# FFN of an encoder kernel: one 512-column product for both parts of the moving operand, and a down projection in two halves of its columns

## Chip, cores and metric

The kernel runs on one core of a Trainium2 chip. The metric is the device time of one execution in microseconds (us), the median of three runs.

## What is computed

An encoder of four layers over 256 tokens of width 1024. Every layer is a half-step SwiGLU FFN, a mixer (attention, convolution, Fourier, gated linear attention in turn) and a second half-step FFN, each with an RMS norm ahead of it; a last norm ends it. The change is in the FFN, which runs eight times:

```python
D_MODEL, SEQ, DEPTH, D_FF = 1024, 256, 4, 2816
def _swiglu(h, w1, w3, w2):
    return (jax.nn.silu(h @ w1) * (h @ w3)) @ w2
for i in range(DEPTH):
    h = h + 0.5 * _swiglu(_rmsnorm(h, norm_g[i, 0]), ffn_w1[i, 0], ffn_w3[i, 0], ffn_w2[i, 0])
    h = h + mix(_rmsnorm(h, norm_g[i, 1]))
    h = h + 0.5 * _swiglu(_rmsnorm(h, norm_g[i, 2]), ffn_w1[i, 1], ffn_w3[i, 1], ffn_w2[i, 1])
return _rmsnorm(h, final_norm_g)
```

## The kernel before

Activations lie transposed on the chip, features on the partitions and 256 tokens along the free dimension. Each float32 matrix operand is split into a high part and a low part (type fp32r), and a product of two of them is three matmuls: high times high, high times low, low times high (`mm3`). The weight is the stationary operand (128x128), the activation the moving one (256 columns), and the three accumulate into the same 256 columns of a PSUM bank.

Weights come in blocks of 1 MB (128x2048), in the order in which they are used (`plan`). SP starts the transfer of a block into one of four `raw` buffers; `split_block` makes the high part `wh` on ACT (L151) and the low part `wl` on DVE (L154), into one of four pairs. `done` notes that a block's products are issued, and `pump(n)` then splits up to n further blocks into the pairs that come free. The order of each engine's work is the order in which the code calls it; nothing reorders it.

An FFN (`ffn`) walks over 11 groups of 256 of the 2816 hidden features. For a group i it multiplies x by a block of w1 (`A`) and one of w3 (`B`), 96 matmuls each at 48 per block, the result of a block being one of four rotating PSUM banks `ab`. `evac_a` multiplies A by R (1/rms of each token) on DVE (L441) and takes silu on ACT (L442); `evac_b` multiplies B by R (L447), multiplies the two (L448) and splits the result into `gh` (ACT, L517) and `gl` (DVE, L518). The down projection of group i-1 follows group i (`DOWN_AFTER`; the last three come at the end), 48 matmuls into four banks D that hold all 1024 output columns through the whole FFN. `down_final` finishes the four D banks one after the other, and `close_pair` adds each to the residual h (L261), scales it by the norm's gain into the next stage's x (`normed`) and squares it (`square`).

R needs the sum over all of x, so it comes late: `stats(True)` sums on PE in the middle of group 0 (L389 reads it), and `newton_rsqrt` takes three Newton steps of three DVE instructions (L354 to L356). After the first two DVE instructions of it two blocks are split, the low part of one on DVE, that of the other on POOL (`eng=nc.gpsimd`). The stage of the convolution mixer uses the same `stats(True)`.

Of the kernel before, what the change touches and what calls it, by code (L numbers as in the profile page):

```python
# [20 lines left out]

DOWN_AFTER = {i: i - 1 for i in range(1, NG - 2)}
DOWN_AFTER[NG - 1] = NG - 3
# [17 lines left out]
class Enc:  # L41
    def __init__(self, ctx, tc, a, stages):
        self.ctx, self.tc, self.nc, self.a = ctx, tc, tc.nc, a
        self.stages = stages
        P = lambda name, bufs=1, **kw: ctx.enter_context(tc.tile_pool(name=name, bufs=bufs, **kw))
        self.const = P("const")
        self.wp = P("wp")
        self.hp = P("hp")
        self.ev = None
        self.ps = P("ps", space=PSUM)  # L50
        self.dram = P("dram", space=bass.MemoryType.DRAM)
        self.nm = 0

# [8 lines left out]
    def ab(self):  # L62
        return self.ps.tile([128, 512], F32, tag="ab", name=self.name("ab"), bufs=4)

    def dbank(self, j):
        return self.ps.tile([128, 512], F32, tag=f"D{j}", name=self.name(f"D{j}"), bufs=1)
# [6 lines left out]

    def mm3(self, out, l, r, start, stop, passes=(0, 1, 2)):
        (lh, ll), (rh, rl) = l, r
        for p in passes:
            self.mm(out, (lh, lh, ll)[p], (rh, rl, rh)[p], start and p == 0, stop and p == 2)
# [6 lines left out]
    def plan(self):  # L84
# [58 lines left out]
    def split_block(self, between=None, eng=None):  # L143
# [5 lines left out]
        wh = self.sb(self.wp, [128, 2048], F32R, "wh", NW)  # L149
        wl = self.sb(self.wp, [128, 2048], F32R, "wl", NW)  # L150
        self.nc.scalar.activation(wh, raw, AF.Copy)  # L151
        if between:
            between()
        (eng or self.nc.vector).tensor_tensor(wl, raw, f32(wh), ALU.subtract)  # L154
        self.wsp[b] = (wh, wl)
        self.dma_block()

    def take(self, key):
# [3 lines left out]
        wh, wl = self.wsp.pop(b)  # L162
        r = lambda t: t.rearrange("p (a b) -> p a b", a=self.blocks[b][1])
        return r(wh), r(wl)
# [17 lines left out]
    def setup(self):  # L182
# [9 lines left out]
        for b in first:  # L192
            self.raw[b] = self.sb(self.wp, [128, 2048], F32, "raw", NR)
            self.wsp[b] = (self.sb(self.wp, [128, 2048], F32R, "wh", NW), self.sb(self.wp, [128, 2048], F32R, "wl", NW))
# [19 lines left out]
        for j in range(4):  # L214
            self.normed(j)
            s = slice(512 * j, 512 * j + 512)
            for b in first:
                wh, wl = self.wsp[b]
                self.split(self.raw[b][:, s], wh[:, s], wl[:, s])
# [6 lines left out]
        while self.nsplit < NW:  # L226
            self.split_block(eng=nc.gpsimd)
# [19 lines left out]
    def close_pair(self, j, P, scale, bias=None):  # L247
        nc = self.nc
        h = self.h[j]
        P3 = P.rearrange("p (c n) -> p c n", c=2)  # L250
        if self.unperm:
            assert bias is None
            hn = self.sb(self.ev, [128, 2, 256], F32, "sl", 2)
            for c in range(2):
                nc.vector.scalar_tensor_tensor(hn[:, c].rearrange("p (m a) -> p a m", a=4),
                                               P3[:, c].rearrange("p (a m) -> p a m", a=4), float(scale),
# [3 lines left out]
        elif bias is None:  # L260
            nc.vector.scalar_tensor_tensor(h, P3, float(scale), h, ALU.mult, ALU.add)  # L261
        else:
            for c in range(2):
                nc.vector.scalar_tensor_tensor(h[:, c], P3[:, c], bias[c], h[:, c], ALU.add, ALU.add)
# [8 lines left out]
    def normed(self, j, h=None):  # L273
# [3 lines left out]
        if self.nstage < len(self.stages):  # L277
            xh = self.sb(self.hp, [128, 2, 256], F32R, f"xh{j}")
            xl = self.sb(self.hp, [128, 2, 256], F32R, f"xl{j}")
# [5 lines left out]
            self.xn[j] = (xh, xl)  # L285
        else:

            y = f32(self.sb(self.hp, [128, 2, 256], F32R, f"xh{j}"))
# [5 lines left out]
    def square(self, j, h=None, before_split=None):  # L294
# [17 lines left out]
        if j == 3:  # L312
# [5 lines left out]
            if self.row_norm():  # L318
                self.nsq = [self.sb(self.hp, [128, 256], F32R, "R", 2) for _ in range(2)]
                self.split(self.acc[:, 0], *self.nsq)  # L320
# [16 lines left out]
    def xk(self, k, t=None):  # L337
        xh, xl = self.x[k // 2]
        if t is None:
            return xh[:, k % 2, :], xl[:, k % 2, :]  # L340
        return xh[:, k % 2, 128 * t:128 * t + 128], xl[:, k % 2, 128 * t:128 * t + 128]

    def newton_rsqrt(self, y, r, shape, tag, bufs=2, pool=False):
# [37 lines left out]
    def stats(self, row=False, scale=1.0):  # L381

        if row:
# [6 lines left out]
            self.newton_rsqrt(y, self.R, [128, 256], "nR", 1, self.nstage > 0)  # L390
            return
# [24 lines left out]

    def ffn(self, l, s):
# [4 lines left out]
        g = {}  # L422

        def up(i, names, hook={}):

            ws = [self.take((n, i)) for n in names]
            ps = [self.ab() for _ in names]
            for k in range(8):
                for w, p in zip(ws, ps):
                    for c in range(2):  # L430
                        sl = slice(128 * c, 128 * c + 128)
                        self.mm3(p[:, 256 * c:256 * c + 256], (w[0][:, k, sl], w[1][:, k, sl]), self.xk(k),
                                 start=k == 0 and c == 0, stop=k == 7)
                if k in hook:
                    hook[k]()
            self.done(len(names))
            return ps

        def evac_a(A):
            sl = self.sb(self.ev, [128, 2, 256], F32, "sl", 2)  # L440
            nc.vector.tensor_tensor(sl, self.v2(A), self.Rb(), ALU.mult)  # L441
            nc.scalar.activation(sl, sl, AF.Silu)  # L442
            return sl

        def evac_b(i, sl, B):
            br = self.sb(self.ev, [128, 2, 256], F32, "br", 2)
            nc.vector.tensor_tensor(br, self.v2(B), self.Rb(), ALU.mult)  # L447
            nc.vector.tensor_tensor(br, sl, br, ALU.mult)  # L448
            gh = self.sb(self.ev, [128, 2, 256], F32R, "gh", 3)
            gl = self.sb(self.ev, [128, 2, 256], F32R, "gl", 3)  # L450
            self.split(br, gh, gl)
            g[i] = (gh, gl)

        self.down_begin()
        first = self.nstage == 0
        A0, B0 = up(0, ("w1", "w3"), {7 if first else 4: lambda: self.stats(True)})
        for i in range(1, NG):
            A, = up(i, ("w1",))
            if i == 1:
                s0 = []  # L460
                self.pump(1, between=lambda: s0.append(evac_a(A0)), eng=nc.gpsimd if first else None)
                evac_b(0, s0[0] if s0 else evac_a(A0), B0)
            sl = evac_a(A)
            self.pump()
            if i == 4 and pre:
                self.pre = pre()
            B, = up(i, ("w3",))
            evac_b(i, sl, B)
            self.pump()
            if i in DOWN_AFTER:  # L470
                self.down_add(self.take(("w2", DOWN_AFTER[i])), g.pop(DOWN_AFTER[i]))
                self.done()
                if i < NG - 1:
                    self.pump()
        w = [self.take(("w2", i)) for i in (NG - 2, NG - 1)]
        self.down_final([(w[0], g[NG - 2]), (w[1], g[NG - 1])], 0.5)
        self.done(2)
        self.pump_end()
        self.close_stage(st)

# [7 lines left out]
    def dmm(self, w, g, d, k, stop=False, passes=(0, 1, 2)):  # L488
        if self.D4 is None:
# [4 lines left out]
                 (w[0][:, k, 128 * d:128 * d + 128], w[1][:, k, 128 * d:128 * d + 128]),  # L494
                 (g[0][:, k], g[1][:, k]), start=self.dfirst[j], stop=stop, passes=passes)
# [20 lines left out]
    def split(self, src, hi, lo):  # L516
        self.nc.scalar.activation(hi, src, AF.Copy)  # L517
        self.nc.vector.tensor_tensor(lo, src, f32(hi), ALU.subtract)  # L518
# [38 lines left out]
    def mix1(self):  # L557
# [12 lines left out]
        def pw1(i, names=("pa", "pg"), hook={}):  # L570
            ws = [self.take((n, i)) for n in names]
            ps = [self.ab() for _ in names]
            for k in range(8):
                for w, p in zip(ws, ps):
                    for c in range(2):
                        sl = slice(128 * c, 128 * c + 128)
                        self.mm3(p[:, 256 * c:256 * c + 256], (w[0][:, k, sl], w[1][:, k, sl]), self.xk(k),
# [78 lines left out]
        A0, G0 = pw1(0, hook={4: lambda: self.stats(True)})  # L656
# [84 lines left out]
        nn = self.sb(ev, [128, 4, 2, 256], F32R, "zs", 3)  # L741
        for i in range(4):
            if i < 2:
                hi, lo = (self.sb(self.hp, [128, 2, 256], F32R, f"x{t}{i}") for t in "hl")
            else:
                hi, lo = nn[:, 2 * i - 4], nn[:, 2 * i - 3]
# [9 lines left out]
            if i:  # L756
                for c in range(2):
                    self.split(zc[i][:, c], hi[:, c], lo[:, c])
            g.append((hi, lo))
# [20 lines left out]
    def mix2(self):  # L780
# [10 lines left out]
        def s1(g, banks):  # L791
            for t in range(2):
                for kk in range(2):
                    self.mm3(banks[t][:, 0:260], self.xk(2 * g + kk, t), tuple(half(w, kk) for w in cs),
                             start=kk == 0, stop=kk == 1)
            return banks

        def e1(g, banks):
            for t in range(2):
                h = self.sb(self.ev, [128, 260], F32R, f"a{g}{t}h")  # L800
                l = self.sb(self.ev, [128, 260], F32R, f"a{g}{t}l")
# [3 lines left out]
                ab[g][t] = (h, l)  # L805

        def s2(j):
# [3 lines left out]
            for c in range(2):  # L811
                for t in range(2):
                    for q in range(2):
# [3 lines left out]
                        h, l = ab[j][t]  # L817
                        self.mm3(p[:, 256 * c:256 * c + 256], (h[:, o:o + 128], l[:, o:o + 128]),
                                 (cs[0][:, t, r], cs[1][:, t, r]), start=n == 0, stop=t == 1 and q == 1)
# [688 lines left out]
```

## Time and profile before

| | us |
|---|---|
| median of three runs (2006.0 to 2008.27) | 2007.27 |
| the profiled execution, its own time | 2007.91 |
| its span, first to last instruction | 2006.1 |
| PE busy | 1959.9 |
| DVE busy | 1280.1 |
| ACT busy | 891.0 |

The profile page gives busy time by engine. A matmul's row is longer than the distance between the starts of two neighbours, since one begins while the last still drains; so the pace of PE is read from starts, not from durations. An idle time in a row of the timeline stands in brackets with the engine and line that ended it. PEclk in a table of stretches is the share of the full clock that was granted.

### The profile page before, as it was taken

The numbers are of one execution on the slowest core, as the hardware profiler recorded it, in microseconds if no ns is written. First come the engines' busy times: TensorE is split into PE (matmuls) and PEld (weight loads), VectorE is DVE, ScalarE is ACT, GpSimd is POOL, SyncE is SP. The second block draws the span as 40 slices with busy tenths as digits, with TensorE's granted clock in tenths as the row PEclk, the third lists the DMA queues.
The fourth block names the chain that finished last, engine by engine and source line by source line (L and its number), as shares of the span: only waits on it lengthen the run. The fifth ranks groups of instructions, "written<-read, shape, count | busy, mean of one in ns | idle before, by whom it ended". The sixth has DMA issues, their size and how long they took to land.

```text
span 2006.1 us, 36900 instructions
## 1 busy us (share of the span) xinstructions
PE 1959.9 (98%) x16496; PEld 1926.2 (96%) x16496; DVE 1280.1 (64%) x1396; ACT 891.0 (44%) x921; POOL 90.2 (4%) x65
## 2 busy tenths in 40 slices
PE   7999999999999999899999999999999999999998
PEld 7999999999999997699999999999999999999998
DVE  6655667755675567775557655765576556767554
ACT  4433545543444443544334434443344445754433
POOL 2000000000060000000001000000010000001000
PEclk9999999999999999899999999999999999999999
DMA  6555533455445434145544553455446553334551
GB/s 233 213 188 186 185 145 127 166 191 181 156 180 202 178 143 163 51 179 192 184 161 181 190 189 127 156 202 188 175 152 227 184 185 148 127 127 168 192 186 43
DMA packets 48671, 338.59 MB, mean 169 GB/s; under 512 B 5568, under 2 KB 5744, under 8 KB 8192
## 3 DMA queue, kind: packets, MB, share of 16 engines
q1 hardware_dynamic: 47952, 335.11, 45.8%
q8 instruction: 129, 2.11, 0.4%
q0 software_dynamic: 560, 1.12, 0.2%
q14 instruction: 30, 0.25, 0.0%
HBM read 335.16 MB, written 1.05 MB: 168 GB/s over the span
## 4 chain that ended last, share of the span: by engine, by line
PE 89%; DVE 7%; ACT 2%; issue 1%; DMA 1%; SPq 0%; DVEq 0%; ACTq 0%
PE ab L69 57%; PE D L69 31%; DVE wl L154 2%; DVE nRt L354 1%; DVE zc L643 1%; ACT wh L151 1%; DMA raw<-in_ffn_w_dram 0%; DVE R L356 0%; DVE nRu L355 0%; PE D L72 0%; DVE nRu L348 0%; DMA h<-in_x_dram 0%; PE ab L72 0%; DVE R L518 0%; ACT zc L753 0%
## 5 line engine op out<-in xcount | busy, mean ns | idle before, releaser
L154 DVE TENSOR_TENSOR wl<-raw,wh 128x2048 fp32r<-128x2048 f32 x305 | 696.7, 2294 | 409.7 <-ACT wh L151 409.4
L69 PE MATMUL ab<-xh,wh 128*128 128x256 f32 x3200 | 911.9, 285 | 7.7 <-ACT wh L517 7.7
L69 PE MATMUL ab<-xh,wl 128*128 128x256 f32 x3200 | 909.3, 284 | 6.2 <-DVE wl L154 6.2
L69 PE MATMUL ab<-xl,wh 128*128 128x256 f32 x3200 | 908.9, 284 | 0.0
L151 ACT ACTIVATE wh<-raw 128x2048 fp32r<-128x2048 f32 x315 | 595.2, 1904 | 111.5 <-issue 84.9
L69 PEld LDWEIGHTS ab<-xh,wh 128*128 128x128 f32 x3200 | 617.9, 193 | 13.7 <-ACT wh L517 7.7
L69 PEld LDWEIGHTS ab<-xh,wl 128*128 128x128 f32 x3200 | 617.5, 193 | 6.9 <-DVE wl L154 6.6
L69 PEld LDWEIGHTS ab<-xl,wh 128*128 128x128 f32 x3200 | 617.9, 193 | 0.0
L69 PE MATMUL D<-gh,wh 128*128 128x256 f32 x1408 | 396.9, 282 | 6.5 <-ACT gh L517 6.5
L69 PE MATMUL D<-gl,wh 128*128 128x256 f32 x1408 | 400.3, 284 | 1.9 <-DVE gl L518 1.9
L69 PE MATMUL D<-gh,wl 128*128 128x256 f32 x1408 | 399.2, 284 | 0.0
L69 PEld LDWEIGHTS D<-gh,wh 128*128 128x128 f32 x1408 | 269.1, 191 | 7.5 <-ACT gh L517 7.5
L69 PEld LDWEIGHTS D<-gl,wh 128*128 128x128 f32 x1408 | 265.3, 188 | 3.0 <-DVE gl L518 2.9
L69 PEld LDWEIGHTS D<-gh,wl 128*128 128x128 f32 x1408 | 265.8, 189 | 0.0
L442 ACT ACTIVATE sl<-sl 128x512 f32<-128x512 f32 x88 | 55.6, 632 | 349.8 <-DVE sl L441 349.7
L517 ACT ACTIVATE gh<-br 128x512 fp32r<-128x512 f32 x88 | 55.6, 632 | 338.1 <-DVE br L448 338.1
L441 DVE TENSOR_TENSOR sl<-ab,R 128x512 f32<-128x512 f32 x88 | 60.6, 689 | 78.2 <-PE ab L69 77.5
L154 POOL TENSOR_TENSOR wl<-raw,wh 128x2048 fp32r<-128x2048 f32 x10 | 51.6, 5164 | 1216.1 <-ACT wh L151 774.6
L518 DVE TENSOR_TENSOR gl<-br,gh 128x512 fp32r<-128x512 f32 x88 | 61.4, 698 | 61.4 <-ACT gh L517 61.4
L282 ACT ACTIVATE xh<-h,cols 128x256 fp32r<-128x256 f32 x88 | 39.9, 500 | 73.9 <-DVE h L261 61.8
L447 DVE TENSOR_TENSOR br<-ab,R 128x512 f32<-128x512 f32 x88 | 60.6, 688 | 13.5 <-PE ab L69 13.5
L448 DVE TENSOR_TENSOR br<-sl,br 128x512 f32<-128x512 f32 x88 | 61.4, 697 | 4.9 <-ACT sl L442 1.4
(446 smaller groups left out, 1495.4 us busy)
## 6 DMA issues: line engine op xcount, KB each, us to landing
raw<-in_ffn_w_dram SPq DMA_DIRECT2D x262, 1024.0 KB, 4.8
raw<-in_attn_w_qk_dram SPq DMA_DIRECT2D x12, 1024.0 KB, 4.8
raw<-in_conv_w_pw_dram SPq DMA_DIRECT2D x12, 1024.0 KB, 4.8
raw<-in_gla_w_in_dram SPq DMA_DIRECT2D x12, 1024.0 KB, 4.9
raw<-in_attn_w_v_dram SPq DMA_DIRECT2D x6, 1024.0 KB, 4.8
raw<-in_fnet_w_dram SPq DMA_DIRECT2D x4, 1024.0 KB, 4.8
raw<-in_gla_w_o_dram SPq DMA_DIRECT2D x4, 1024.0 KB, 4.8
raw<-in_ffn_w_dram SPq DMA_DIRECT2D x8, 256.0 KB, 6.5
```

What stands on the lines that cost most here:

```text
L69: return self.nc.tensor.matmul(out, lhsT, rhs, start=start, stop=stop, skip_group_check=True)
L151: self.nc.scalar.activation(wh, raw, AF.Copy)
L154: (eng or self.nc.vector).tensor_tensor(wl, raw, f32(wh), ALU.subtract)
L282: nc.scalar.activation(xh[:, c], h[:, c], AF.Copy, scale=g[c])
L354: nc.vector.tensor_tensor(t, r, r, ALU.mult)
L441: nc.vector.tensor_tensor(sl, self.v2(A), self.Rb(), ALU.mult)
L442: nc.scalar.activation(sl, sl, AF.Silu)
L447: nc.vector.tensor_tensor(br, self.v2(B), self.Rb(), ALU.mult)
L448: nc.vector.tensor_tensor(br, sl, br, ALU.mult)
L517: self.nc.scalar.activation(hi, src, AF.Copy)
L518: self.nc.vector.tensor_tensor(lo, src, f32(hi), ALU.subtract)
L643: nc.vector.scalar_tensor_tensor(o, x, w, o, ALU.mult, ALU.add)
```

## The change

A weight's high part is loaded once and multiplies both parts of x (or of g) in one matmul of 512 moving columns, whose result is a high half and a low half of one PSUM bank; the low part times the high x adds 256 columns into the high half (`wide`). The two halves are added when the bank is read: ACT copies one half to SBUF (`parts`), DVE adds the other (`add`). A block of 256 features thus takes two banks where it took one. PSUM is two fixed halves of four banks; w1 has two banks (PA) and w3 two (PB), and the down projection has the other four, which is half of its columns. So the gated values `g` of all 11 groups stay on the chip (11 buffers), the first 512 columns are accumulated between the groups, two groups to a block, and the last 512 after them, into the four banks of PA and PB; then the roles of the halves are swapped (`lower`). `w2` is laid out for it in the host's arrays, still 11 blocks of 1 MB.

`R` is no longer needed to free a bank, so the Newton steps are spread between other instructions (`steps`). Silu's input and output are both multiplied by R, so w3's result isn't. POOL splits no blocks any more. `close_pair` adds two halves, one after the other. The other stages use the same banks through `ab` and `dbank`, and `mm3` as before.

```diff
@@ class Enc
     def ab(self):
-        return self.ps.tile([128, 512], F32, tag="ab", name=self.name("ab"), bufs=4)
+        self.nab = (self.nab + 1) % 4
+        while self.nab in self.held:
+            self.nab = (self.nab + 1) % 4
+        return self.bank(self.lower, self.nab)
+    def two(self, half, n):
+        return self.banks[half][n].rearrange("p (c q n) -> p c q n", c=2, q=2)
+    def pair(self, pool, shape, tag, bufs=1):
+        return self.sb(pool, [shape[0], 2, *shape[1:]], F32R, tag, bufs)
@@ def plan
-                    if i in DOWN_AFTER:
-                        add(("w2", DOWN_AFTER[i]), w2[DOWN_AFTER[i]], 2)
-                for i in (NG - 2, NG - 1):
-                    add(("w2", i), w2[i], 2)
+                    if i and i % 2 == 0:
+                        add(("w2", 0, i // 2 - 1), w2[i // 2 - 1], 4)
+                add(("w2",), w2[2 * NP], 2)
+                for i in range(NP):
+                    add(("w2", 1, i), w2[NP + i], 4)
@@ def setup
-        while self.nsplit < NW:
-            self.split_block(eng=nc.gpsimd)
+        self.pend = NW - self.nsplit
@@ def close_pair
-            nc.vector.scalar_tensor_tensor(h, P3, float(scale), h, ALU.mult, ALU.add)
+            for p in P:
+                nc.vector.scalar_tensor_tensor(h, p, float(scale), h, ALU.mult, ALU.add)
@@ def newton_rsqrt
-        if pool:
-            self.pump(1)
-            self.pump(1, eng=nc.gpsimd)
-        for n in range(3):
+        def step():
             nc.vector.tensor_tensor(t, r, r, ALU.mult)
             nc.vector.scalar_tensor_tensor(u, t, -0.5, y, ALU.mult, ALU.mult)
             nc.vector.scalar_tensor_tensor(r, u, 1.5, r, ALU.add, ALU.mult)
+        for _ in range(3 - later):
+            step()
+        return [step] * later
@@ def ffn
+    def wide(self, p, c, w, k, x, start, stop):
+        self.mm(p[:, c, 0], w[:, 1, k], x[:, 0], start, False)
+        self.mm(p[:, c], w[:, 0, k], x, False, stop)
...
+        def parts(P, tag):
+            t = self.sb(self.ev, [128, 2, 256], F32, tag, 2)
+            nc.scalar.activation(t, P[:, :, 1], AF.Copy)
+            return t
+        def add(t, P):
+            nc.vector.tensor_tensor(t, t, P[:, :, 0], ALU.add)
...
+        for n, ks in enumerate(cuts):
+            if n == len(cuts) - 1:
+                if not first:
+                    self.pump(1)
+                up(wa, PA, ks[:2])
+                if first:
+                    break
+                steps = self.stats(True)
+                up(wa, PA, ks[2:])
+            else:
+                up(wa, PA, ks)
+                up(wb, PB, ks)
+        self.done()
+        sl0 = parts(PA, "sl")
+        add(sl0, PA)
+        up(wb, PB, ks)
+        self.done()
...
+        steps.pop(0)()
+        br0 = parts(PB, "br")
+        steps.pop(0)()
+        add(br0, PB)
+        self.pump(held)
+        steps.pop(0)()
         for i in range(1, NG):
-            A, = up(i, ("w1",))
+            take_up("w1", i, PA)
+            sl = parts(PA, "sl")
             if i == 1:
...
+            else:
+                self.pump(1, between=lambda: (add(sl, PA), times_r(sl)))
+                silu(sl)
...
+            take_up("w3", i, PB)
+            br = parts(PB, "br")
+            self.pump(1, between=lambda: (times_r(sl), add(br, PB)))
+            gate(i, sl, br)
+            if i % 2 == 0:
+                p = i // 2 - 1
+                if i == NG - 1:
+                    break
+                self.half_add(self.take(("w2", 0, p)), [g[2 * p], g[2 * p + 1]], 0, p == 0)
...
+        p = NP - 1
+        self.half_add(self.take(("w2", 0, p)), [g[2 * p], g[2 * p + 1]], 0)
+        w = self.take(("w2",))
+        self.begin_close()
+        for j in range(2):
+            self.half_mm(w, [g[NG - 1]], 0, j, stop=True)
+            self.half_close(0, j)
+        self.lower = 1 - self.lower
+        for j in range(2):
+            self.half_mm(w[:, :, :, 512:], [g[NG - 1]], 1, j, start=True)
...
+        for p in range(NP):
+            self.pump(1)
+            w = self.take(("w2", 1, p))
+            if p < NP - 1:
+                self.half_add(w, [g[2 * p], g[2 * p + 1]], 1)
+        for j in range(2):
+            self.half_mm(w, [g[2 * p], g[2 * p + 1]], 1, j, stop=True)
+            self.half_close(1, j)
```

Three places show what moves; all three are in the second FFN of the third layer. First PE, at the start of the w1 block of group 1; `xh`, `xl`, `wh`, `wl` are the parts of x and of the block, `x` and `w` the pairs. Before:

```order
L69 MATMUL ab_15666<-xh_1594_15410,wh_15609 128x256
L69 MATMUL ab_15666<-xl_1595_15411,wh_15609 128x256
L69 MATMUL ab_15666<-xh_1594_15410,wl_15610 128x256
L69 MATMUL ab_15666<-xh_1594_15410,wh_15609 128x256
L69 MATMUL ab_15666<-xl_1595_15411,wh_15609 128x256
L69 MATMUL ab_15666<-xh_1594_15410,wl_15610 128x256
```

After:

```order
L81 MATMUL P_69<-x_949_11762,w_12154 128x256
L81 MATMUL P_69<-x_949_11762,w_12154 128x512
L81 MATMUL P_69<-x_949_11762,w_12154 128x256
L81 MATMUL P_69<-x_949_11762,w_12154 128x512
L81 MATMUL P_69<-x_949_11762,w_12154 128x256
L81 MATMUL P_69<-x_949_11762,w_12154 128x512
```

Three matmuls of 256 columns became one of 256 and one of 512.

Second DVE, from where it reads the sum of squares. Before, from L389 on (the POOL split stands beside L354 on POOL's own row):

```order
L389 TENSOR_SCALAR R_15599<-D_1616_15601 128x256
L348 TENSOR_SCALAR nRu_15606<-R_15599 128x256
L349 TENSOR_SCALAR R_15600<-nRu_15606 128x256
L154 TENSOR_TENSOR wl_15610<-raw_15215,wh_15609 128x2048
L354 TENSOR_TENSOR nRt_15605<-R_15600 128x256
L355 SCALAR_TENSOR_TENSOR nRu_15606<-nRt_15605,R_15599 128x256
L356 SCALAR_TENSOR_TENSOR R_15600<-nRu_15606,R_15600 128x256
```

After (L170 is the low part of a block, L465 is `add`):

```order
L170 TENSOR_TENSOR w_12051<-raw_11841,w_12051 128x2048
L406 TENSOR_SCALAR R_12064<-P_71 128x256
L363 TENSOR_SCALAR nRu_12070<-R_12064 128x256
L364 TENSOR_SCALAR R_12065<-nRu_12070 128x256
L465 TENSOR_TENSOR sl_12081<-sl_12081,P_69 128x512
L367 TENSOR_TENSOR nRt_12069<-R_12065 128x256
L368 SCALAR_TENSOR_TENSOR nRu_12070<-nRt_12069,R_12064 128x256
L369 SCALAR_TENSOR_TENSOR R_12065<-nRu_12070,R_12065 128x256
```

One split moved ahead of the sum, and reading PA moved in between.

Third DVE again, in group 1, with what follows the Newton steps. Before:

```order
L441 TENSOR_TENSOR sl_15718<-ab_15537,R_15600 128x512
L154 TENSOR_TENSOR wl_15716<-raw_15335,wh_15715 128x2048
L447 TENSOR_TENSOR br_15724<-ab_15538,R_15600 128x512
L448 TENSOR_TENSOR br_15724<-sl_15718,br_15724 128x512
L518 TENSOR_TENSOR gl_15728<-br_15724,gh_15727 128x512
L441 TENSOR_TENSOR sl_15731<-ab_15666,R_15600 128x512
```

After (L468 is `times_r`, L474 the gate, L623 the low part of g):

```order
L465 TENSOR_TENSOR sl_12149<-sl_12149,P_69 128x512
L468 TENSOR_TENSOR sl_12081<-sl_12081,R_12065 128x512
L468 TENSOR_TENSOR sl_12149<-sl_12149,R_12065 128x512
L170 TENSOR_TENSOR w_12154<-raw_11915,w_12154 128x2048
L468 TENSOR_TENSOR sl_12081<-sl_12081,R_12065 128x512
L474 TENSOR_TENSOR br_12103<-sl_12081,br_12103 128x512
L623 TENSOR_TENSOR g_12163<-br_12103,g_12163 128x512
L170 TENSOR_TENSOR w_12166<-raw_11952,w_12166 128x2048
L468 TENSOR_TENSOR sl_12149<-sl_12149,R_12065 128x512
L465 TENSOR_TENSOR br_12203<-br_12203,P_70 128x512
L170 TENSOR_TENSOR w_12205<-raw_12054,w_12205 128x2048
```

Between two reads of PA and PB there now stand two splits and five other instructions, where `ab` gave each block a bank of its own.

## Rows read from the trace of the kernel before

**Rows 1.** The page: span, and each engine's busy time with its instructions.

```profile
span 2006.1 us, 36900 instructions
PE 1959.9 (98%) x16496; PEld 1926.2 (96%) x16496; DVE 1280.1 (64%) x1396; ACT 891.0 (44%) x921; POOL 90.2 (4%) x65
```

**Rows 2.** The page: shares of the chain that ended last.

```profile
PE 89%; DVE 7%; ACT 2%; issue 1%; DMA 1%; SPq 0%; DVEq 0%; ACTq 0%
```

**Rows 3.** That chain in order of time: start us, us, engine and tile, instructions.

```profile
376.04 7.39 PE D L69 x47
...
400.70 11.51 PE ab L69 x96
```

**Rows 4.** Timeline of PE in the fourth mixer: start us, us, what.

```profile
1714.73 0.39 PE L69 MATMUL ab<-la00l,lst 128*128 128x512 f32 x1
...
1715.43 0.60 PE L72 MATMUL ab<-ident,kT 128*128 128x128 f32 x4
...
1716.10 0.40 PE L69 MATMUL D<-la01l,lst 128*128 128x512 f32 x1
...
1716.80 0.28 PE L69 MATMUL D<-tri,la00h 128*128 128x256 f32 x1
```

**Rows 5.** The same view earlier: 24 products with 64-column weights, first and next after.

```profile
1685.69 0.28 PE L69 MATMUL ab<-xh,wah 128*64 128x256 f32 x1
...
1688.50 0.61 PE L69 MATMUL D<-ident,rc 128*128 128x128 f32 x4
```

**Rows 6.** Stretches, FFN 2 to 8: us, busy by engine, PEclk, DMA share, GB/s.

```profile
349.50:544.50 195.00, 192.79 (x1589) 191.99 (x1588) 123.69 (x111) 83.46 (x73) 6.11 (x3) 0.99 0.48 175
544.50:738.96 194.46, 192.28 (x1588) 191.88 (x1587) 123.78 (x109) 80.46 (x68) 34.21 (x30) 0.99 0.49 180
857.66:1052.77 195.11, 192.00 (x1588) 191.80 (x1587) 119.27 (x105) 79.20 (x66) 4.71 (x1) 0.99 0.48 175
1052.77:1244.92 192.15, 190.77 (x1588) 190.36 (x1587) 120.33 (x108) 81.43 (x72) 5.98 (x1) 1.00 0.50 180
1286.13:1481.16 195.03, 191.91 (x1589) 191.71 (x1588) 118.89 (x103) 80.32 (x66) 4.61 (x1) 0.99 0.48 174
1481.16:1673.30 192.14, 190.78 (x1589) 190.38 (x1588) 121.01 (x108) 81.59 (x71) 11.82 (x11) 1.00 0.51 186
1803.13:1996.48 193.35, 191.96 (x1599) 191.56 (x1598) 117.16 (x107) 79.04 (x70) 5.31 (x1) 1.00 0.42 150
```

**Rows 7.** Timeline of PE at the first pause of FFN 2.

```profile
375.31 0.39 PE L69 MATMUL D<-gh,wh 128*128 128x256 f32 x1 [1.76 <-ACT gh L517]
376.04 0.49 PE L69 MATMUL D<-gl,wh 128*128 128x256 f32 x1 [0.34 <-DVE gl L518]
```

**Rows 8.** Timeline of PE at that of FFN 8.

```profile
1827.62 0.39 PE L69 MATMUL D<-gh,wh 128*128 128x256 f32 x1 [1.05 <-ACT gh L517]
```

**Rows 9.** Timeline of DVE ahead of it.

```profile
1813.97 4.85 DVE L354 TENSOR_TENSOR nRt<-R 128x256 f32<-128x256 f32 x1
1818.86 0.42 DVE L355 SCALAR_TENSOR_TENSOR nRu<-nRt,R 128x256 f32<-128x256 f32 x1
...
1819.78 0.43 DVE L354 TENSOR_TENSOR nRt<-R 128x256 f32<-128x256 f32 x1
```

**Rows 10.** Timeline of POOL there.

```profile
1813.23 5.31 POOL L154 TENSOR_TENSOR wl<-raw,wh 128x2048 fp32r<-128x2048 f32 x1 [134.50 <-ACT wh L151]
```

**Rows 11.** Groups of DVE by line: busy us, mean ns, idle before.

```profile
L154 DVE TENSOR_TENSOR wl<-raw,wh 128x2048 fp32r<-128x2048 f32 x305 | 696.7, 2294 | 409.7 <-ACT wh L151 409.4
...
L441 DVE TENSOR_TENSOR sl<-ab,R 128x512 f32<-128x512 f32 x88 | 60.6, 689 | 78.2 <-PE ab L69 77.5
```

**Rows 12.** Groups of ACT.

```profile
L151 ACT ACTIVATE wh<-raw 128x2048 fp32r<-128x2048 f32 x315 | 595.2, 1904 | 111.5 <-issue 84.9 <-PE ab L69 18.9 <-PE D L69 6.9
L442 ACT ACTIVATE sl<-sl 128x512 f32<-128x512 f32 x88 | 55.6, 632 | 349.8 <-DVE sl L441 349.7
```

**Rows 13.** What PE waited for: us in total, times, longest.

```profile
PE D L69 <- issue: 4.2, 1, 4.2
```

More of the change, by code (lines that the diff above doesn't have):

```diff
@@ L20 @@
 EPS = 1e-6
-DOWN_AFTER = {i: i - 1 for i in range(1, NG - 2)}
-DOWN_AFTER[NG - 1] = NG - 3
+NP = NG // 2
 NR = 4
@@ L52, in __init__ @@
         self.nm = 0
+        self.banks = [[self.ps.tile([128, 1024], F32, name=f"P{i}{n}") for n in range(2)] for i in range(2)]
+        self.lower, self.nab, self.held = 0, 3, []
     def name(self, s):
@@ L422, in ffn @@
         g = {}
[L424 to L437, printed above, removed]
@@ L454, in ffn, with up, take_up @@
-        self.down_begin()
-        first = self.nstage == 0
-        A0, B0 = up(0, ("w1", "w3"), {7 if first else 4: lambda: self.stats(True)})
+        self.sqtag = ("br", 2)
+        up_half = self.lower
+        PA, PB = (self.two(up_half, n) for n in range(2))
+        def up(w, P, ks=range(8)):
+            for k in ks:
+                for c in range(2):
+                    self.wide(P, c, w[:, :, :, 128 * c:128 * c + 128], k, self.xk(k), k == 0, k == 7)
+        def take_up(n, i, P):
+            up(self.take((n, i)), P)
+            self.done()
@@ new lines, in ffn @@
+        first = self.nstage == 0
+        wa, wb = self.take(("w1", 0)), self.take(("w3", 0))
+        cuts = [range(2 * n, 2 * n + 2) for n in range(4)] if first else [range(4), range(4, 8)]
+        for n, ks in enumerate(cuts):
[10 more added lines that the diff above has]
+                up(wb, PB, ks)
@@ L478, in ffn, with half_mm @@
+        for j in range(2):
+            self.half_mm(w, [g[2 * p], g[2 * p + 1]], 1, j, stop=True)
+            if j and self.nstage >= len(self.stages):
+                self.fin_transpose(2)
+            self.half_close(1, j)
+        self.done()
         self.pump_end()
         self.close_stage(st)
+        self.sqtag = ("sq", 2)
+    def half_mm(self, w, gs, half, j, start=False, stop=False):
+        P = self.two(1 - self.lower, j)
+        ks = [(n, k) for n in range(len(gs)) for k in range(2)]
+        for n, k in ks:
+            for c in range(2):
+                o = 256 * j + 128 * c
+                self.wide(P, c, w[:, :, :, o:o + 128], 2 * n + k, gs[n][:, :, k], start and (n, k) == ks[0],
+                          stop and (n, k) == ks[-1])
@@ L482, with half_add, half_close @@
+    def half_add(self, w, gs, half, start=False):
+        for j in range(2):
+            self.half_mm(w, gs, half, j, start)
+    def half_close(self, half, j):
+        P = self.two(1 - self.lower, j)
+        self.close_pair(2 * half + j, [P[:, :, 1], P[:, :, 0]], 0.5)
     D4 = None
@@ L793, in s1 @@
                 for kk in range(2):
-                    self.mm3(banks[t][:, 0:260], self.xk(2 * g + kk, t), tuple(half(w, kk) for w in cs),
-                             start=kk == 0, stop=kk == 1)
+                    x, w = self.xk(2 * g + kk, t), [half(cs[:, q], kk) for q in range(2)]
+                    for n, (a, b) in enumerate(((0, 0), (1, 0), (0, 1))):
+                        self.mm(banks[t][:, 0:260], x[:, a], w[b], kk == 0 and n == 0, kk == 1 and n == 2)
             return banks
@@ L1061, in mix3, with bank @@
         bkn = [0]
-        def bank():
+        def bank(hold=False):
             bkn[0] += 1
```

219 lines of the change are left out of this document (110 added, 109 removed).

## The prediction

> **What bounds the kernel now.** I read the busy times first: PE is busy for 98% of the span, DVE for 64%, ACT for 44% [rows 1], and the chain that ended last is 89% PE [rows 2]. DMA moves weights at about half of what its engines could [rows 6]. So the time is the number of matmuls times their pace, plus the pauses of PE. The pace comes from starts: 96 products in 11.51 us are 119.9 ns each [rows 3], for 256 moving columns and a 128-column weight. An FFN has 22 up blocks of 16 triples and 11 down blocks of 16, so 528 triples or 1,584 products, and 2 for the norm: 1,586 x 0.12 = 190.3 us. The stretches [rows 6] show what is above that: 4.7, 4.2, 4.8, 1.9, 4.7 and 1.8 us in FFN 2 to 7; the stretch of FFN 8 holds the kernel's end too, so I give it 1.8, as in the two others with a full clock. Together 23.9 us.
>
> Where they come from: PE waits for the first gated value of group 0, 1.76 and 0.34 us in FFN 2 [rows 7], 1.05 us in FFN 8 [rows 8]. Ahead of that DVE sits 4.85 us in a Newton instruction that takes 0.43 otherwise [rows 9], while POOL splits a block for 5.31 us [rows 10]. The longer pauses cost twice: in FFN 2 the 47 products behind the pause take 7.39 us where 5.64 would do, 1.75 us more [rows 3], and PEclk is 0.99 in the four FFNs with over 4 us and 1.00 in the others [rows 6]. So after a pause of about 2 us the clock falls to the lower level for a while, after 1.4 it didn't.
>
> **Term 1, the products.** Two products instead of three, the same 768 columns. The trace has matmuls of 512 columns with 128-column weights: three starts from 1714.73 to 1715.43 and three from 1716.10 to 1716.80, 0.70 us each time, 233.5 ns per product [rows 4]. So a triple goes from 360 to 120 + 233.5 = 353.5 ns: 6.5 ns x 528 x 8 = 4,224 triples = **-27 us**. One bound: with a 64-column weight 256 columns take 2.81 us / 24 = 117 ns [rows 5], so 3 ns are owed to the loading, which a product behind a 512-column one might lose: 9.5 ns, -40 us. The other: no row has a moving operand in two pieces of 256, and if it streams as two products (240 ns) the gain is 0. I take 6.5, from the row that has the width. So this is a small gain in pace, not a third.
>
> The Trainium skill (TensorE: Matmul & The Clock Gate, Back-to-back issue gap) gives a warm gap of N/2.4 + 2.5 ns: 109 for 256 columns, 216 for 512, so a triple would go from 328 to 325 ns, an estimate of -11 us in all. The trace disagrees in both levels, 120 and 233.5, and the sum goes by the trace; by the page it would end 16 us later.
>
> **Term 2, the start of FFN 2 to 8.** POOL's split and its stall of 4.4 us go; the split that POOL did (one of 2.2 us between starts) is DVE's. But each block's read now takes one more DVE instruction (six of 0.69 us a group: add, R, R, add, gate, split of g; before four: R, R, gate, split) and an ACT copy of 0.63 [rows 11, 12], and PA has to be read before the next w1 block, 5.66 us after its own end. I followed the rows of the changed order with these durations (DVE 2.25 a split, 0.72 for 128x512, 0.46 for a Newton instruction, ACT 1.9 and 0.65), from the last product of the FFN before, t = 0. DVE closes the last pair and forms x until 5.7, splits until 9.4, reads the sum and PA until 11.2; PE asks for PA at 11.6, no pause. Two Newton steps, PB and a split take until 16.95, and PE needs that block (w3 of group 1) at 17.2, no pause. The last step ends at 18.35; then add, two R, and the split of w1's group 2, which has to wait for its high part because silu stands ahead of it on ACT: until 24.6, while PE is done at 22.9: **pause of 1.75**. Then the gate of group 0, the next split until 30.9, R and the add of PB until 32.35, with PE done at 30.35: **pause of 2.05**. From there the down block between the groups (5.66 us of PE) gives DVE room, 20 us of work for 28 us of PE per two groups, so no more pauses. 7 x 3.8 = 26.6 against the 23.9 of now: **+3 us**. Bounds: each of the two figures is some 1 us uncertain, so 7 x 1.8 to 7 x 5.8, -11 to +17.
>
> **Term 3, the end.** The last group's value is needed one down block (16 triples, 5.66 us) after its w3 block; before, 60 products or 7.2 us lay between and no row shows a wait there. The chain: drain 0.3, copy 0.65, high part 1.9, low part 2.25 (it stands ahead of the gate on DVE), gate 0.7, high g 0.65, low g 0.7 = 7.2 us with the gaps, PE's first need of the high g at 6.55. So 0.9 and then 0.6 us of pause, 8 x 1.5 = **+12 us**. Bounds 0 and 8 x 2.5 = 20.
>
> **Term 4, the clock.** The pauses of FFN 2 to 8 now cost 4 low stretches, which term 2's 23.9 contains. Of the new ones 2.05 is about the size that did it, 1.75 and 1.5 below. A fall behind the first is mostly repaid, since PE then asks later and the second pause shrinks. I take 4 falls of 1.75: **+7 us**; bounds 0 and 15 falls, 26 us.
>
> **Term 5, the convolution stage.** The same stall of DVE by POOL ends in a wait of 4.2 us [rows 13]. DVE's split takes 2.2 instead of 4.4, so about 2 less, and 1 us less at the low clock: **-3 us** (0 to -6). **Term 6**: the closing of the last pair has a second instruction of 0.69 us [rows 11] with nothing behind it: +0.7; in the other stages it lies beside the 5.7 us of products that need only older parts of x. In the first FFN the loads set the start, as before, and I put 0. The second half of the columns costs no wait that I can find: its split blocks are two ahead, five splits in 28 us; its banks are read 3 us before they are needed. SP starts as many transfers of the same size, in the same pace, each behind the same kind of free buffer: 0.
>
> **The sum**: -27 + 3 + 12 + 7 - 3 + 0.7 = -7.3. The profiled execution took 2007.91 (span 2006.1 and 1.8 around it), 0.6 above the median: 2007.9 - 7.3 = 2000.6, less 0.6 is **2000 us**.
>
> **Rivals.** (a) *The clock falls at nearly every long pause.* For it: pauses of 2 us did that in FFN 2 [rows 7]; against it: 1.4 didn't in FFN 8 [rows 8]. Without falls the sum is -14.3; each costs 1.75, so from 8 falls on it is a draw and from 11 the kernel is slower by over 0.2%; 15 (each second pause and each end) give +12, **2019 us**. (b) *The widening doesn't pay*, because a moving operand in two pieces goes at two products' pace: term 1 is 0, **2027 us**. For it: no row has two pieces. Against it: 512 columns in one piece are measured. (c) *Only loading is saved*: a product costs its columns, and what a triple loses is one weight load that shows, the 3 ns between 117 and 120 [rows 3, 5]: 4,224 x 3 = 12.7 us, 14 less than term 1, **2014 us**; for it, that PE's other rows have no product of 512 between two of 256, against it the 233.5. The gap rule of the page named above says nearly the same, 2.5 ns a triple. (d) *The pauses don't open*, DVE being 2 us faster through the start than I follow it: terms 2 to 4 become -24 + 8 x 0.5 = -20 and term 1 stays: **1958**; half of the start's pauses, with the end's as I have them and no fall of the clock, **1979**. For it: DVE waits 3.2 us for high parts in my walk, which ACT might give earlier. (e) *A 512-column product at the pace of the full clock alone*, 512 / 2.4 = 213 ns: 20 ns a triple more, 85 us, **1915**; no row has it.
>
> **How the numbers follow.** Forecast 1990 to 2009: 0.5. (a) 0.17, (b) 0.08, (c) 0.06, (d) 0.16, (e) 0.03. About 0.2%, 4 us, can be told from no change, so faster means below 2003.3 and slower above 2011.3. Faster: 0.35 of the forecast's 0.5, with (d) and (e) 0.54. Same: 0.13 of it and 0.05 of (a): 0.18. Slower: 0.02 of it, the rest of (a), (b) and (c): 0.28. The range reaches past (a) and to (d)'s nearer case with 7 us for what its terms leave open: 1972 to 2021, and leaves out (e), the far end of (d) and most of (b). The forecast's own range is 1990 to 2009.
>
> **What would show it.** Starts in a stretch of up blocks: a triple in 353 to 354 ns, 11.3 us for two blocks; 360 means (b), 333 means (e). In FFN 3 to 8 a wait of PE for DVE (the low part of w1's group 2, then the add of PB), about 1.8 and 2 us, and one for the g of group 10 of about 1 us on ACT and 0.6 on DVE. No Newton instruction over 0.5 us beside a POOL split. PEclk 1.00 or 0.99 by FFN tells (a). An FFN should take about 186.9 + 5.3 = 192 us, and 194 with a fall. The forecast is wrong if the pauses are twice these or nothing, or if the splits themselves fall behind in the second half of the columns.

## The result and the profile after

The changed kernel takes 2094.2 us (median of 4 runs, 2093.38 to 2096.42) against 2007.31 for the kernel before (4 runs beside it): a ratio of 1.0435, 95% interval 1.0417 to 1.0453. It is slower by 87 us where 2000 us was forecast, and outside the range of 1972 to 2021.

Lines of the page of the profile after: span, busy time by engine, then PE and its clock in 40 slices, then the chain that ended last, and PE's largest group.

```profile
span 2092.4 us, 28814 instructions
...
PE 1949.4 (93%) x12272; PEld 1712.3 (82%) x12272; DVE 1390.8 (66%) x1614; ACT 978.3 (47%) x1097; POOL 34.5 (2%) x55
...
PE   7999978899989998799999999999999997889998
...
PEclk9999989999999999899999999999999998999999
...
PE 79%; DVE 11%; ACT 6%; issue 3%; DMA 0%; SPq 0%; ACTq 0%; DVEq 0%
...
L81 PE MATMUL P<-x,w 128*128 128x256 f32 x6976 | 1183.4, 330 | 80.8 <-DVE qk L1017 17.7
```

A quarter of the matmuls is gone and PE is busy for 10.5 us less, but it is idle for 143 us where it was for 46 [rows 1]. The chain has less PE and more DVE and ACT [rows 2]. Of the eleven slices of PE with a 7 or an 8, eight hold part of a mixer; the others are the first, the last and one in the third FFN. The first releaser of PE's largest group is `qk`, which belongs to the attention mixer.

Stretches (from the first product of a stage to that of the next) say it in numbers. First the five stretches of FFNs in the kernel after: us, PE busy, granted clock, DMA share, GB/s.

```profile
7.64:200.75 193.11, 188.25 (x1058) 1.00 0.59 211
379.24:763.92 384.68, 374.49 (x2118) 0.99 0.51 181
901.04:1278.86 377.82, 370.91 (x2118) 1.00 0.51 184
1333.12:1710.70 377.58, 370.47 (x2119) 1.00 0.52 186
1890.45:2081.27 190.82, 186.62 (x1068) 1.00 0.42 149
sum 1524.01, PE 1490.74; mean PE 298.15
```

The same five stretches of the kernel before sum to this.

```profile
sum 1556.05, PE 1535.55; mean PE 307.11
```

Then the four mixers, before.

```profile
207.75:349.50 141.75, 141.44 (x1231) 136.96 (x1229) 95.27 (x156) 70.09 (x97) 0.00 (x0) 1.00 0.43 159
738.96:857.66 118.70, 108.38 (x1186) 93.56 (x1185) 92.12 (x160) 57.19 (x94) 6.47 (x7) 0.93 0.31 114
1244.92:1286.13 41.21, 41.21 (x350) 41.21 (x349) 28.34 (x41) 22.41 (x32) 0.00 (x0) 1.00 0.42 154
1673.30:1803.13 129.83, 129.82 (x1022) 119.16 (x1021) 88.93 (x172) 82.73 (x125) 0.55 (x2) 1.00 0.35 133
sum 431.49, PE 420.85 PEld 390.89 DVE 304.67 ACT 232.42 POOL 7.02; mean PE 105.21 PEld 97.72 DVE 76.17 ACT 58.11 POOL 1.76
```

And after.

```profile
200.75:379.24 178.49, 150.64 (x1230) 144.06 (x1228) 97.55 (x160) 72.25 (x101) 0.00 (x0) 0.94 0.33 121
763.92:901.04 137.12, 111.78 (x1185) 95.76 (x1184) 89.73 (x159) 56.47 (x92) 0.42 (x6) 0.88 0.26 93
1278.86:1333.12 54.26, 46.62 (x350) 45.71 (x348) 27.41 (x42) 21.11 (x32) 0.00 (x0) 0.91 0.27 98
1710.70:1890.45 179.75, 146.18 (x1021) 130.71 (x1020) 91.61 (x175) 84.08 (x126) 0.55 (x2) 0.90 0.26 94
sum 549.62, PE 455.22 PEld 416.23 DVE 306.30 ACT 233.92 POOL 0.97; mean PE 113.80 PEld 104.06 DVE 76.57 ACT 58.48 POOL 0.24
```

So the FFNs, which the change is about, gain 32.0 us, and the mixers, whose matmuls are the same in number, lose 118.1. Of that, 34.4 us is longer PE work (455.22 against 420.85: the granted clock is 0.88 to 0.94 there where it was 1.00, and 0.93 in the second), and 83.8 is more idle time of PE (94.4 against 10.6). DVE and ACT do the same work as before in them, within 2 us.

What PE waits for shows in the timeline of the attention mixer after (start us, us, engine, line, operation; in brackets the idle time before and its releaser). Line L1017 makes PE wait 17.7 us in all, four times, three of them for about 5.7; this is one of the three.

```profile
302.08 3.13 PE L81 MATMUL P<-x,w 128*128 128x256 f32 x24
...
305.99 1.89 ACT L167 ACTIVATE w<-raw 128x2048 fp32r<-128x2048 f32 x1
306.32 0.49 DVE L1064 TENSOR_SCALAR e<-e,rsm 128x512 f32<-128x512 f32 x1
...
307.92 2.29 DVE L170 TENSOR_TENSOR w<-raw,w 128x2048 fp32r<-128x2048 f32 x1 [1.11 <-ACT w L167]
310.13 0.68 DVE L1017 TENSOR_TENSOR qk<-P,Rqk 128x512 f32<-128x512 f32 x1
...
310.87 2.93 PE L81 MATMUL P<-x,w 128*128 128x256 f32 x12 [5.66 <-DVE qk L1017]
```

PE stands idle from 305.2 to 310.87. In the built program the products at 310.87 write the second bank of the tile P11 and `qk` reads its first; in the rows `qk` stands on DVE behind a softmax and the split of a weight block. The two touch no common bank, but they touch one tile. In the changed kernel `ab` and `dbank` hand out the halves of two-bank tiles, and the framework makes its waits by tile: some 70 matmuls of the built program, all in the mixers, wait for a read of the other bank of their tile (counted in the program, not in the trace). Before, where each bank is a tile, there is none.

### The profile page after: what moved, and what is told of

It is laid out like the page before. It is cut to its first block, busy times and chain, and to the rows that moved or that the text cites. A ratio compares the mean times of both kernels' runs of the same rounds, so it can differ in the third digit from the quotient of the medians.

```text
span 2092.4 us, 28814 instructions
## 1 busy us (share of the span) xinstructions
PE 1949.4 (93%) x12272; PEld 1712.3 (82%) x12272; DVE 1390.8 (66%) x1614; ACT 978.3 (47%) x1097; POOL 34.5 (2%) x55
## 4 chain that ended last, share of the span: by engine, by line
PE 79%; DVE 11%; ACT 6%; issue 3%; DMA 0%; SPq 0%; ACTq 0%; DVEq 0%
PE P L81 79%; DVE w L170 4%; ACT w L167 3%; DVE sl L468 1%; DVE zc L748 1%; DVE s L1046 1%; DVE br L474 1%; PE P L84 0%; DVE m L1049 0%; DMA h<-in_x_dram 0%; DVE h L277 0%; DVE sl L465 0%; DVE br L465 0%; ACT sl L471 0%; DVE g L623 0%
## 5 line engine op out<-in xcount | busy, mean ns | idle before, releaser
L81 PE MATMUL P<-x,w 128*128 128x256 f32 x6976 | 1183.4, 330 | 80.8 <-DVE qk L1017 17.7
L81 PEld LDWEIGHTS P<-x,w 128*128 128x128 f32 x6976 | 1040.2, 192 | 219.8 <-DVE qk L1017 18.5
L170 DVE TENSOR_TENSOR w<-raw,w 128x2048 fp32r<-128x2048 f32 x315 | 719.7, 2293 | 273.1 <-ACT w L167 272.9
L167 ACT ACTIVATE w<-raw 128x2048 fp32r<-128x2048 f32 x315 | 597.6, 1906 | 65.2 <-PE P L81 44.8
L81 PE MATMUL P<-g,w 128*128 128x256 f32 (+1 forms) x2816 | 504.2, 337 | 7.1 <-ACT g L622 4.3
L81 PEld LDWEIGHTS P<-g,w 128*128 128x128 f32 x2816 | 433.3, 187 | 73.7 <-ACT g L622 6.9
L468 DVE TENSOR_TENSOR sl<-sl,R 128x512 f32<-128x512 f32 x176 | 121.7, 695 | 2.5
L81 PE MATMUL P<-w,x 128*128 128x256 f32 (+1 forms) x720 | 95.7, 294 | 8.4 <-ACT Em L1334 3.4
L623 DVE TENSOR_TENSOR g<-br,g 128x512 fp32r<-128x512 f32 x88 | 61.2, 695 | 61.5 <-ACT g L622 61.5
L81 PEld LDWEIGHTS P<-w,x 128*128 128x128 f32 x720 | 92.7, 202 | 10.3 <-ACT Em L1334 3.8
L465 DVE TENSOR_TENSOR sl<-sl,P 128x512 f32<-128x512 f32 x88 | 60.2, 684 | 47.0 <-ACT sl L461 46.7
L465 DVE TENSOR_TENSOR br<-br,P 128x512 f32<-128x512 f32 x88 | 60.3, 686 | 43.7 <-ACT br L461 43.7
L474 DVE TENSOR_TENSOR br<-sl,br 128x512 f32<-128x512 f32 x88 | 60.6, 689 | 0.3
L1017 DVE TENSOR_TENSOR qk<-P,Rqk 128x512 f32<-128x512 f32 x12 | 8.3, 688 | 32.6 <-PE P L81 32.6
```

The lines of the kernel that those rows point to most:

```text
L81: return self.nc.tensor.matmul(out, lhsT, rhs, start=start, stop=stop, skip_group_check=True)
L167: self.nc.scalar.activation(w[:, 0], raw, AF.Copy)
L170: (eng or self.nc.vector).tensor_tensor(w[:, 1], raw, f32(w[:, 0]), ALU.subtract)
L465: nc.vector.tensor_tensor(t, t, P[:, :, 0], ALU.add)
L468: nc.vector.tensor_tensor(t, t, self.Rb(), ALU.mult)
L623: self.nc.vector.tensor_tensor(p[:, 1], src, f32(p[:, 0]), ALU.subtract)
```

## The experiments

Theory 1 was this: false waits for the neighbour bank. Theory 2: the fixed rotation of `ab`, which takes the place of "whichever is free", asks for a bank too soon. Theory 3: something else that the diff does in the mixers (splits moved from POOL to DVE, other neighbours of the norm).

**e1, one-bank tiles in the mixers.** A pool of PSUM is closed and opened at each border between an FFN and a mixer, with other tiles at the same addresses.

```diff
+        n, m = (2, 1024) if wide else (4, 512)
+        self.banks = [[ps.tile([128, m], F32, name=self.name(f"P{i}{j}")) for j in range(n)] for i in range(2)]
...
+                self.psum(st[0] == "ffn")
```

> The changed kernel, with PSUM laid out in two-bank tiles in the FFNs and in eight one-bank tiles, at the same addresses, in the mixers. Theory 1 (in the mixers PE waits for readers of the other bank of a two-bank tile): the mixers go from 568 us back to the 451 us that they took before, the FFNs keep their 1524 us; 2094 - 117 = 1977 us, 1968 to 1990. Theory 2 (the banks are given out in a fixed rotation instead of as they come free, so that one is asked for too soon): nothing changes, 2085 to 2100. Theory 3 (the other edits in the mixers: splits that POOL did are on DVE, the conv stage's row norm has other neighbours): 2085 to 2100 too.

Measured: 1993.53 us, ratio to before 0.9936 (0.9921 to 0.9951). That is 100.7 us under the changed kernel, which theories 2 and 3 exclude, but 16 us short of theory 1's number and 3.5 us outside its range. The mixers' stretches sum to this.

```profile
sum 451.49, PE 426.18 PEld 393.75 DVE 308.66 ACT 232.96 POOL 0.97; mean PE 106.54 PEld 98.44 DVE 77.16 ACT 58.24 POOL 0.24
```

They are 20 us above the kernel before (my "451 us before" counted the kernel's start and end among the mixers; 431.5 is right). And at the border from attention to the FFN behind it PE waits for the last pair's close.

```profile
PE P L94 <- DVE h L291: 4.9, 1, 4.9
```

`h<-P` is the last read of the mixer's PSUM (349.57 to 350.25 us), and the FFN's first product starts at 350.40, though it doesn't need that read: with one-bank tiles everywhere (e4) PE waits for nothing at this border. So this edit takes the false waits away and brings waits at the borders; that they are the 16 us is borne out by e4, below.

**e2, the kernel before, with only the tiles changed.** The mixers' eight banks become halves of four two-bank tiles in the changed kernel's rotation; the FFNs stay as they were.

> The kernel before, with the mixers' eight banks as halves of four two-bank tiles, given out in the changed kernel's rotation; the FFNs keep one-bank tiles. Theory 1: the mixers alone lose what they lose in the changed kernel, 2007 + 117 = 2124 us, 2100 to 2140. Theory 2: the same, but then the next kernel is as slow. Theory 3: 2003 to 2012.

Its control has the same rotation over one-bank tiles.

> The kernel before, with one-bank tiles everywhere, given out in the changed kernel's fixed rotation; it differs from the run before it in the width of the mixers' tiles alone. Theory 1: 2003 to 2012 us. Theory 2: 2100 to 2140. Theory 3: 2003 to 2012.

Measured: 2140.77 us (ratio 1.0670, 1.0652 to 1.0687) and 2007.09 (0.9999, 0.9990 to 1.0008). The rotation costs nothing, the pairing 134 us (just past its range), in a kernel without any other part of the change. Its attention mixer waits for `qk` as the changed kernel's does (us in total, times, longest):

```profile
PE P L88 <- DVE qk L928: 17.7, 4, 5.7
```

The mixers of the paired one:

```profile
sum 557.04, PE 459.45 PEld 419.25 DVE 305.49 ACT 235.18 POOL 5.58; mean PE 114.86 PEld 104.81 DVE 76.37 ACT 58.80 POOL 1.40
```

That is 125.6 us above before. How much of it, and of the other 8 us, are border waits as in the run above, no run tells apart. Theories 2 and 3 are out.

**e3, the changed kernel, neighbours apart.** One line: banks that are handed out one after the other lie in different tiles.

```diff
-        return self.banks[half][j // 2][:, 512 * (j % 2):512 * (j % 2) + 512]
+        return self.banks[half][j % 2][:, 512 * (j // 2):512 * (j // 2) + 512]
```

> The changed kernel, two-bank tiles everywhere, but banks that are asked for one after the other come from different tiles (one line). Theory 1: a bank's neighbour was asked for two steps earlier instead of one, so most of its reads are over: half to four fifths of the 117 us come back, 2000 to 2036 us, with waits left. Theories 2 and 3: 2085 to 2100.

Measured: 2036.37 us (1.0154, 1.0132 to 1.0175), at the upper edge of theory 1's range: 58 of the 118 us come back, and the mixers' stretches sum to 493.12 us. The program now has more such waits, some 90 against some 70. So it isn't their number that sets the cost; what fits is how recent the read is that they wait for, which was argued ahead of the run and not measured wait by wait.

**e4, one-bank tiles everywhere.** Here no tile is wider than a bank and none changes at a border; the FFNs read each bank by itself.

```diff
-            nc.scalar.activation(t, P[:, :, 1], AF.Copy)
+            for c in range(2):
+                nc.scalar.activation(t[:, c], P[c][:, 1], AF.Copy)
...
-            nc.vector.tensor_tensor(t, t, P[:, :, 0], ALU.add)
+            for c in range(2):
+                nc.vector.tensor_tensor(t[:, c], t[:, c], P[c][:, 0], ALU.add)
```

> The changed kernel with eight one-bank tiles everywhere; in the FFNs each read of a pair of banks becomes two reads of 256 columns. No tiles change at a stage's border, where the run with one-bank mixers alone shows PE waits of 5.2, 3.5 and five of 1.3 to 2.2 us. Theory 1 (false waits for the neighbour bank; the 16 us missing in that run are the borders): mixers 451 us, FFNs 1524 + some 4 for the added reads: 1979 us, 1972 to 1986. Rival (the 16 us are a cost of the change in the mixers beside the false waits): 1990 to 1997.

Measured: 1969.39 us (0.9817, 0.9802 to 0.9832), 125 under the changed kernel and 3 us below the range that I expected, since the right figure for the mixers is 431.5. They are back:

```profile
sum 428.56, PE 420.12 PEld 390.49 DVE 298.22 ACT 226.65 POOL 0.97; mean PE 105.03 PEld 97.62 DVE 74.56 ACT 56.66 POOL 0.24
```

At the same place of the attention mixer PE now runs on: the 24 products of 302.08 and the 12 that waited until 310.87 are one row of 36. The last 12 start at 291.91, 5.1 us before `qk` (here L1031) reads the bank beside theirs:

```profile
288.94 4.57 PE L81 MATMUL P<-x,w 128*128 128x256 f32 x36
...
294.78 2.29 DVE L170 TENSOR_TENSOR w<-raw,w 128x2048 fp32r<-128x2048 f32 x1 [1.12 <-ACT w L167]
...
296.99 0.69 DVE L1031 TENSOR_TENSOR qk<-P,Rqk 128x512 f32<-128x512 f32 x1
```

The added reads cost the FFNs nothing (1521.96 us in sum against 1524.01). The Trainium skill (PSUM — Partial Sum Buffer, PSUM bank collisions raise a hardware error) asks for guards by bank, or by bank and quadrant. Waits by bank are what this kernel has, and here they are 121 us cheaper in the mixers than waits by tile.

**e5, the width of the products.** e4 with each 512-column product made as two.

```diff
-        self.mm(p[c], w[:, 0, k], x, False, stop)
+        for q in range(2):
+            self.mm(p[c][:, q], w[:, 0, k], x[:, q], False, stop)
```

> The kernel of the run before it, with each 512-column product of the FFNs made as two of 256 columns into the same bank (1.5 times the products, the same columns). If a triple of 120 ns starts is 360 ns and the changed triple 349 (its trace), 4,224 triples cost 46 us, less some 6 that the pauses give back as PE arrives later: e4 + 40, +30 to +50. By the price of the prediction (353.5 ns): + 27, less the same, + 21. Rival (c) of the prediction (3 ns a triple): + 13 or less.

Measured: 2013.20 us (1.0035, 1.0022 to 1.0048), 43.8 above. The chain of waits has the stretch between two pauses of one FFN, the same 335 triples: start us, us, products; first one-bank tiles everywhere, then narrow.

```profile
874.16 116.64 PE P L81 x670
```

```profile
889.26 120.85 PE P L81 x1005
```

348.2 ns a triple against 360.7: the width alone, with the one product and the one weight load that it saves, is worth 12.5 ns, beyond the prediction's bound of 9.5. The 43.8 us lie in the range that follows from the trace; the prediction's own price (+21) and rival (c) (+13 or less) are out.

**e6, e8 and e9, the pauses of the FFNs.** Three edits on top of e4, each on top of the one ahead. First (e6), in an FFN's last group the gate stands ahead of a block's split on DVE and ACT.

```diff
+                times_r(sl)
+                add(br, PB)
+                gate(i, sl, br)
+                self.pump(1)
```

> e4 with one thing moved: in the last group of an FFN the gate stands ahead of the split of a weight block on DVE and ACT. The pause of PE at the end of each FFN (0.81 + 0.61 us over the pace) goes: 8 x 1.4 to 1.7 = 11 to 14 us under e4. If the moved split is late for its own product instead, PE waits there and it is e4 again.

Measured: 1961.26 us (0.9777, 0.9762 to 0.9791), 8.1 less: below the range, in the right direction. The waits for g are gone from FFN 4 where e4 had 0.3 and 0.3 us, so there was less to win than in the changed kernel. Second (e8), the two splits at the start have their high parts ahead of silu and of the gate on ACT (the first of the two is shown).

```diff
-                add(sl, PA)
-                times_r(sl0)
-                silu(sl0)
-                self.pump(1, between=lambda: times_r(sl))
+                self.pump(1, between=mid)      # mid: add, times_r(sl0), silu(sl0), times_r(sl)
```

> e6 with the start of the FFNs reordered: the high parts of the two splits after the first groups stand ahead of silu and of the gate on ACT, so that DVE doesn't wait for them (1.9 and 1.1 us in the trace of e1). The pauses of 1.4 to 1.7 us and 1.6 to 1.8 shrink by 3.0 us in seven FFNs: 21 us under e6, 12 to 24. If DVE's own work is the bound and not its waits, it stays within 3 us of e6.

Measured: 1937.95 us (0.9666, 0.9647 to 0.9685), 23.3 less. FFN 4 to 7 then run without a pause (the row of FFN 4 and 5; that of 6 and 7 has 368.88 us):

```profile
829.08:1197.82 368.74, 368.74 (x2118) 1.00 0.52 189
```

So DVE waited there for ACT's copies, not for want of time. The third (e9) finishes a block's first bank before its second.

> e8 with the up blocks in another order: all products of a block's first bank, then all of its second, so that with one-bank tiles the first bank's reads can run beside the second's products. If the reads at a block's end are what PE still waits for (1.3, 2.4 and 1.6 us in FFN 2 and 3, 1.4 in FFN 1), 3 to 8 us under e8. If DVE's order decides (the reads stand behind a split there), within 3 us of e8.

Measured: 1939.61 us (0.9664, 0.9647 to 0.9682), no different. What is left of the pauses, in FFN 1 to 3, isn't mended by an earlier read of the first bank.

**e10, POOL's split alone, in the kernel before.**

```diff
-            self.pump(1, eng=nc.gpsimd)
+            self.pump(1)
```

> The kernel before with one thing changed: the split that POOL did during a row norm is DVE's. Term 2 and term 5 of the prediction rest on this: DVE's Newton instruction falls from 4.85 to 0.45 us, DVE gets 2.25 us of work, so 2.1 us less ahead of the first gated value; PE's pauses there (1.0 to 2.1 us) go in most FFNs with what the clock costs behind them, and 2 us of the conv stage: 1988 to 1999 us. If POOL's split holds nobody up, 2003 to 2012, or more by 2 us per FFN where DVE is late.

Measured: 1991.11 us (0.9921, 0.9905 to 0.9938). The longest `nRt`, 4.87 us before, is 0.84, and FFN 4 to 7 have no pause left:

```profile
852.14:1232.65 380.51, 380.51 (x3174) 1.00 0.49 180
1273.86:1654.37 380.51, 380.51 (x3174) 1.00 0.50 183
```

The Trainium skill (Trainium Architecture — The Big Picture, What this means for kernel authors) says that VectorE and GpSimd share a port that one of them locks. The runs agree as far as they go: without POOL's split the stall of 4.4 us beside it [rows 9, 10] is gone.

## Why the prediction was wrong

**The step that failed is one that is missing.** The part-by-part cost went through the products, the FFN's order on DVE, the row norm and the close of a pair. It has no term for what the diff does to `ab` and `dbank`: every stage takes its banks from them, and the diff makes each of their banks half of a tile. I priced two-bank tiles only where the FFN reads them as a whole, and for the other stages wrote no more than that a second closing instruction "lies beside the 5.7 us of products". None of the five rivals has it either; the three that end slower work by the clock in the FFNs or by the pace of the products. The measured price is +118.1 us: 2094 less 118 is 1976, close to the 1969 of one-bank tiles. Against that kernel the forecast was 31 us too high: 20 are term 1's, and 9 those of terms 2 to 4.

**Term 1, the products: the mechanism right, the size too small.** FFN 4 to 7 run without a pause both in e10 (380.51 us a pair, three products) and in e8 (368.74, two): 5.9 us an FFN, 47 us in eight. I took 27, with a bound at 40. In the starts of the trace after, the product of 512 columns takes about 232 ns (the median) where my row had 233.5 [rows 4], and that of 256 takes 117 where it was 120, as the bound from the 64-column weights had it [rows 5]. Rivals (b), 0, and (c), 13 us, fall with it; so does (e), whose 213 ns no product shows.

**Terms 2 to 4, the pauses and the clock: right in kind, a third too dear.** Above the pace of e10 and e8 the FFNs lose 1556.05 - 8 x 190.26 = 34 us before and 1524.01 - 8 x 184.37 = 49 after: +15 where the three terms gave +22. The four places are those of the prediction, in FFN 4 each 0.3 to 0.65 us shorter than the 1.75, 2.05, 0.9 and 0.6 of the forecast. (The 6.55 us in term 3 is when the high part of g is ready; PE first needs it at 5.66.) What PE waits for in FFN 4 after:

```profile
PE P L81 <- DVE br L465: 1.4, 1, 1.4
PE P L81 <- DVE w L170: 1.2, 1, 1.2
PE P L81 <- ACT g L622: 0.5, 1, 0.5
PE P L81 <- DVE g L623: 0.3, 1, 0.3
```

The clock did not fall behind these: it is 1.00 in FFN 4 to 8. In FFN 3 two of the pauses at the start are longer and there is one more, and there it fell twice:

```profile
588.19 7.40 PE L81 MATMUL P<-x,w 128*128 128x256 f32 x32 [1.81 <-DVE w L170]
596.85 5.91 PE L81 MATMUL P<-x,w 128*128 128x256 f32 x32 [1.26 <-DVE w L170]
604.90 7.42 PE L81 MATMUL P<-x,w 128*128 128x256 f32 x32 [2.14 <-DVE br L465]
```

Behind 1.81 and 2.14 us the 32 products take 1.5 us longer than behind 1.26, at a granted clock of 0.77 against 1.00. So two falls of 1.5 us came where term 4 has four of 1.75, and rival (a)'s number of falls is too high. The "3.2 us for high parts" that I noted as speaking for rival (d) were there to be had, but only once ACT's order was changed (e8).

**Term 5, the convolution stage: right.** -3 forecast; its stretch goes from 118.70 us to 115.76 in e4, and to 115.83 in e10, which takes away POOL's split alone. In the changed kernel the gain is buried under false waits.

**What term 2 took for the cause, POOL's split, was it.** It is worth 16 us by itself (e10), and without it the kernel before has no pause in FFN 4 to 7. So the pauses of the changed kernel are new ones, from reading PA and PB before the next block, and not what is left of the old; e6 and e8 took most of them away. (Between two such reads DVE has two splits and six other instructions; the section on the change says five.)

## What to carry to other kernels

When a buffer is made wider than the unit that an instruction touches, list every user of the buffer, not only those that the change is for: in this framework waits go by the buffer, and two users that share nothing else now wait for each other. Price such a wait by how long the neighbour's reader is queued: here 5.7 us for a read of 0.7, because it stood behind a softmax and a split. Narrow tiles with twice the reads cost nothing measurable, and with them the wide product is worth 47 us; with its pauses closed the kernel takes 1938 us, 3.3% less than before; against the kernel before without POOL's split (e10) it is about 2.6%.

## What the runs showed of the hardware

A moving operand in two separate pieces of 256 columns streams as one of 512: about 232 ns, where one piece of 512 took 233.5 [rows 4]; a 256- and a 512-column product take 348 ns together, against 361 for three of 256. Pauses of PE of 1.2 and 1.4 us in FFN 4 left the granted clock at 1.00; those of 1.81 and 2.14 us in FFN 3 were followed by products at 0.77. In the mixers, with pauses of up to 9 us, it was 0.88 to 0.94, and the 12 products behind one of 5.66 took 2.93 us, 244 ns each at a granted clock of 0.50, the lower of the two levels, where the 36 in one row took 127 each. One thing stays open: in e10 the fourth mixer took 134.42 us instead of 129.83, without a pause of PE and at a granted clock of 0.96. The fall is one stretch, 1677.30 to 1687.55 us, at 0.51; ahead of it and behind it the clock is 1.00, and the kernel before has no fall at that place. No run tells why.

```profile
1654.37:1788.79 134.42, 134.41 (x1023) 0.96 0.35 129
```
